# A shorter recurrence step, its inputs by quarters, and five smaller rearrangements in an attention and state-space kernel

## The chip, the cores and the metric

The kernel runs on one core of a Trainium2 chip. The metric is the time of one execution on the device, in microseconds (us). Three runs of the kernel before gave a median of 1029.72 us (1029.02 to 1033.26).

## What is computed

Two blocks follow each other on 512 tokens of width 1024, all in fp32. The first is a gated block: normalisation, one projection into a short convolution and a dilated attention of 8 heads, an output projection, and a feed-forward part of width 2816. The second mixes a state-space model with a sparse attention:

```python
proj = h @ w_in                       # xa, za, q, k, v, zb, qi, ki, wi, ga, gb
ya = gelu(s5_mixer(xa, ...))          # h_t = abar * h_(t-1) + B u_t;  y_t = Re(C h_t) + D u_t
yb = dsa_mixer(q, k, v, qi, ki, wi)   # each query attends to its top 128 keys
merged = sigmoid(ga) * (glu(ya) * silu(za)) @ w_a_o + sigmoid(gb) * (yb * silu(zb)) @ w_b_o
x = x + gate * (merged @ w_out)
return rms_norm_2(x, final_g)
```

The state-space model has 32 groups of 16 channels with 64 complex states each. Abar, the input and output matrices come from parameters through exp, sin and cos, which the kernel computes itself by polynomials.

## The kernel before, in words

**Products.** Every large product is three matmuls of rounded parts (`mm3`, L186 to 190): high by high, high by low, low by high. Weights come in units of 128x1024, 512 KB each. SP loads a unit (`load_w`, L113), ScalarE makes its high part `wh` (L92), VectorE subtracts to get the low part `wl` (L93); three buffers of each kind exist. A projection of one tile of 128 features takes 24 matmuls of 512 columns.

**Order.** TensorE's order is written out by hand: the program mixes a main thread with a "filler", a generator that gives a few k-steps of a projection each time it is called. The orders of the other engines are set by a scheduler from the program, its priorities and its estimate of times. Each engine executes its own order strictly in sequence.

**Start.** `first_w` loads the first weight unit in two pieces of 128x512; the loop at L330 takes the eight tiles of x in turn, splits them, and loads `ident`, `cm`, `lc` and `gqk` at the fifth of them.

**Feed-forward.** For the first gate tiles, exp, sines and tables of the state-space parameters are computed beside the projections (`beside`, with a rate of side work per k-step). The exponentials run as a chain of 128x48 operations on GpSimd (`ex_q`, `ex_r`), the sines on VectorE (`sc_p`); `snr` (L851) joins them. `table` (L884) makes the tiles `ba` and `ca` for four chunks of 8 groups. `gs` (L596) is the gate tile scaled out of PSUM.

**State space.** `ssm_in` projects xa in four quarters, stores each to `xad` in DRAM, and reads all of it back, transposed, as U in eight DMAs. Time is cut in 64 chunks of 8 tokens. `chunk_in` multiplies U by `bt` for each of four sets of 8 groups, copies the four quarters of each result into H (64 chunks x 2 x 16 complex parts), and then runs the recurrence over the chunks: 63 steps of four GpSimd operations (L1136 to L1140), each step needing the one before. Calls of `next(cin)` place the products between q projections (L1160) and heads (L1236). `chunk_out` copies H, shifted by one chunk, into `hs` (L1171) and multiplies by `ca`/`cat` and `tt`. The copies alternate between ScalarE (L241) and VectorE (L243). They are in the filler behind the gate projections `thb` (L1220), while the main thread runs the attention: scores (L249, L250), `z` on VectorE (L253), the exponential `e` on ScalarE (L257), its scaling (L260), transposes (L301), `pT` (L307), values (L278).

**End.** The last projection and the last norm go by halves of 256 tokens. A norm sums squares (L1359, L1362), takes a root on VectorE in a series of 128x2 operations (`rev`, `rey`, L199 to L207), spreads it over partitions (L231) and multiplies eight tiles of x: the first half on GpSimd (L1374), the second on VectorE (L1376).

Of the kernel before, what the change touches and what calls it, by code (L numbers as in the profile page):

```python
# [9 lines left out]
F = mybir.dt.float32  # L10
R = mybir.dt.float32r
# [7 lines left out]
S = 512  # L19
D = 1024  # L20
P = 128
# [7 lines left out]
RAW = 3  # L29
# [5 lines left out]
class K:  # L35
# [8 lines left out]
    def pool(self, st, name, bufs=1, **kw):  # L44
        if "space" not in kw or kw["space"] == PSUM:
            kw.setdefault("reuse_waits", "tile")
        return st.enter_context(self.tc.tile_pool(name=name, bufs=bufs, **kw))


    def setup(self):  # L50
        nc, a, ctx = self.nc, self.a, self.ctx
        c = self.cpool = self.pool(ctx, "consts")
        self.wpool = self.pool(ctx, "weights")
        self.hpool = self.pool(ctx, "parts")
        self.ps = self.pool(ctx, "psum", space=PSUM)
        self.dram = ctx.enter_context(self.tc.tile_pool(name="scratch", bufs=1, space=DRAM))
        self.ones = c.tile([P, P], F, name="ones")
        self.G.memset(self.ones, 1.0)
        warm = c.tile([P, 1], F, name="warm")
        self.A.activation(warm, self.ones[:, 0:1], AF.Tanh)  # L60
        p = self.tp()
        for _ in range(WARM):
            self.T.matmul(p[:, :P], self.ones, self.ones, start=True, stop=True)
        self.cols = c.tile([P, NCOLS], F, name="cols")
        nc.scalar.dma_start(self.cols, a["cols"])
        self.ident = c.tile([P, P], F, name="ident")
        self.ident_r = c.tile([P, P], R, name="ident_r")
        self.cm = c.tile([P, P], F, name="cm")

    def col(self, name, j):  # L70
        o = COLS[name][0] + j
# [23 lines left out]

    def first_w(self):

        raw = self.wpool.tile([P, 2, S], F, name="raw", tag="raw", bufs=RAW)
        hi = self.wpool.tile([P, 2, S], R, name="wh", tag="wh", bufs=3)
        lo = self.wpool.tile([P, 2, S], R, name="wl", tag="wl", bufs=3)  # L100
        for k in range(2):
            src = self.a["wqkv"]
            ap = bass.AP(tensor=src.tensor, offset=src.offset + k * S, ap=[[2 * S, P], [1, S]])
            self.nc.sync.dma_start(raw[:, k], ap)
            self.A.copy(hi[:, k], raw[:, k])
            self.V.tensor_sub(lo[:, k], raw[:, k], hi[:, k].bitcast(F))
            yield hi, lo

    def load_w(self, name, off, kt, n):
        raw = self.wpool.tile([P, kt, n], F, name="raw", tag="raw", bufs=RAW)  # L110
# [5 lines left out]
    def units(self):  # L116

        def cols(name, c0, c1, kt, n):
            for c in range(c0, c1):
                yield self.split_w(self.load_w(name, c * P * kt * n, kt, n))  # L120
        yield from cols("wqkv", 1, 12, 2, S)
        yield from cols("wconv", 0, 12, 8, P)
        yield from cols("wout", 0, 8, 4, 256)
        yield from cols("wgu", 0, 44, 8, P)
        for n in range(8):
            for k0, kt in ((0, 8), (8, 8), (16, 6)):
                yield self.split_w(self.load_w("wdown", (n * 22 + k0) * P * P, kt, P))
        yield from cols("win2", 0, 5, 8, P)
        yield self.split_w(self.load_w("win2v", 0, 8, 72))
        yield from cols("win2", 5, 29, 8, P)  # L130
        yield from cols("wab", 4, 7, 4, 256)
        yield from cols("wglu", 0, 4, 4, 256)
        yield from cols("wab", 7, 8, 4, 256)
        for c in range(4):
            yield from cols("win2", 29 + 2 * c, 31 + 2 * c, 8, P)
            yield from cols("wab", c, c + 1, 4, 256)
        yield from cols("wout2", 0, 8, 8, P)
# [173 lines left out]
    def mixer(self):  # L311
        nc, a, V, A, G, T = self.nc, self.a, self.V, self.A, self.G, self.T
        st = ExitStack()
        sm = self.pool(st, "smallA")
# [13 lines left out]
        sq = sm.tile([P, S], F, name="sqA", tag="sq")  # L328
        first = self.first_w()
        for k in range(8):  # L330
            if k < 2:
                unit = next(first)
                if k:
                    self.ahead.append(unit)
            x = t1.tile([P, S], F, name="x", tag="x", bufs=2)
            nc.sync.dma_start(x, a["xT"][:, k * S:(k + 1) * S])
            if k in (2, 4):
                self.ahead.append(next(self.stream))
            if k == 4:
                nc.sync.dma_start(self.ident, a["ident"])  # L340
                nc.sync.dma_start(self.cm, a["cm"])
                nc.sync.dma_start(self.lc, a["lc"])
                nc.sync.dma_start(self.gqk, a["gqk"])
            g = self.col("g_mix", k)
            A.activation(xh[k], x, AF.Copy, scale=g)
            V.scalar_tensor_tensor(xl[k], x, g, xh[k].bitcast(F), op0=OP.mult, op1=OP.subtract)
            if k == 0:
                A.activation(sq, x, AF.Square)
            else:
                s2 = t1.tile([P, S], F, name="s2", bufs=2)  # L350
                A.activation(s2, x, AF.Square)
                G.tensor_add(sq, sq, s2)
        self.A.copy(self.ident_r, self.ident)
        self.mod_start()
        gqk = sm.tile([P, 64], F, name="gqk1")
        V.scalar_tensor_tensor(gqk, self.gqk[:, 0], 0.125, self.gqk[:, 1], op0=OP.mult, op1=OP.mult)
        rx = sm.tile([P, 4], F, name="rx")
# [207 lines left out]
    def ffn(self, x1):  # L565
# [13 lines left out]
        xs = []  # L579
# [47 lines left out]
        for j in range(22):  # L627
            if j == 0:
                ws, first = [self.w() for _ in range(3)], [self.acc() for _ in range(3)]
                for js, ks in (((0, 1), range(4)), ((2,), range(4)), ((0, 1, 2), range(4, 8))):  # L630
                    for k in ks:
                        for q in js:
                            self.gemm(first[q], ws[q], xs, [k])
                with self.tc.high_priority(offset=LEAD):
                    r = self.rms(wk, [sq], D, "rf")
                continue
            if j == 1:
                first.append(beside(self.proj(xs), 0.25))
                continue
            if j == 2:  # L640
                pg = beside(self.proj(xs, self.acc2), 0.25)
                with self.tc.high_priority(offset=LEAD):
                    Rf = self.spread(wk, r, wk.tile([P, S], F, name="Rf"))
                pu = beside(self.proj(xs, self.acc2), 0.25)
                finish(0, *first[:2])
                finish(1, *first[2:])
                finish(2, pg, pu)
                continue
            ps = []
            for _ in range(2):  # L650
                t = self.proj(xs)
                ps.append(beside(t, 0.25 if j < 4 else 0.36))
            finish(j, *ps)
            if j > NT1:
                self.advance_mod()
# [140 lines left out]
    def ssm_tables(self, st):  # L796
# [84 lines left out]
        for c in range(4):  # L881
            gs = slice(8 * c, 8 * c + 8)
            def table(x, y, nj, name):
# [3 lines left out]
                sh = [P, 8, nj - 1, 16]  # L887
                pw = lambda z: z[:, 1:nj, gs].rearrange("p j g -> p g j")[:, :, :, None].to_broadcast(sh)
                vb = lambda z: z[:, gs, None, :].to_broadcast(sh)
                A.copy(o[:, :, 0], x[:, gs])  # L890
                V.tensor_mul(o[:, :, 1:], vb(x), pw(pr))
                yield
                V.tensor_mul(t, vb(y), pw(pi))
# [95 lines left out]
    def hybrid(self, xs, second, close, out):  # L989
# [35 lines left out]
        ap = self.pool(aa, "attnE")  # L1025
        ss = ExitStack()
        ssp = self.pool(ss, "ssm", side="right")
        U = ssp.tile([P, 32, 64], F, name="U")
        H = ssp.tile([P, 64, 2, 16], F, name="H")
        s1 = ExitStack()  # L1030
# [37 lines left out]
        def ssm_in():  # L1068
            for j in range(4):
# [1 line left out]
                xp = ssi.tile([P, 8, 64], F, name="xp", bufs=2)  # L1071
                A.copy(xp, p.rearrange("p (c s) -> p s c", s=8))
                nc.sync.dma_start(xad[j], xp.rearrange("p s c -> p (s c)"))
            for j in range(8):
                nc.sync.dma_start(U[16 * j:16 * j + 16], x4[7 - j])


        self.filler = ssm_in()
# [41 lines left out]
        def chunk_in():  # L1120
            for c in range(4):
# [5 lines left out]
                pv = pe.rearrange("p (g e c) -> p e g c", e=2, c=64)  # L1127
                for e in range(2):
                    for ri in range(2):
                        self.copy(H[64 * e:64 * e + 64, :, ri, 4 * c:4 * c + 4].rearrange("p c g -> p g c"),  # L1130
                                  pv[64 * ri:64 * ri + 64, e])
                yield
            for c in range(1, 64):
                m = ssi.tile([P, 2, 2, 16], F, name="hm", bufs=2)
# [1 line left out]
                G.tensor_mul(m, H[:, c - 1, None].to_broadcast([P, 2, 2, 16]),  # L1136
                             self.a8.rearrange("p (w r) g -> p w r g", w=2))
                G.tensor_add(u, m[:, 0], H[:, c])  # L1138
                G.tensor_add(H[:, c, 0], u[:, 0], m[:, 1, 1])  # L1139
                G.tensor_add(H[:, c, 1], u[:, 1], m[:, 1, 0])  # L1140


        def silu2(out, p):
# [6 lines left out]
        for c in range(4):  # L1150
            self.filler = self.proj(xs)
            p = None
            for k in range(8):
# [3 lines left out]
                    p = e.value  # L1157
                if k % 2:
                    next(sel, None)
                if k == 7 and c > 1:  # L1160
                    next(cin, None)
            p = self.run(self.filler) if p is None else p
            q.extend(stack(p, 2 * c, 0.125, ap, "q"))
# [69 lines left out]
        def head(i, h):  # L1233
            for _ in range(2 if i < 3 else 0):
                next(sels[min(i + 1, 2)], None)
            if i == 0 and h < 3:  # L1236
                next(cin, None)
            if h == 0:
                for m in range(i):
# [114 lines left out]
        def norm(e):  # L1354
# [15 lines left out]
                Rs = x3p.tile([P, S // 2], F, name="Rs")  # L1370
                A.copy(Rs, Rl)
            for k in range(8):
                if e == 0:
                    G.tensor_mul(x3[k][:, t], x3[k][:, t], Rs)  # L1374
                else:
                    V.tensor_mul(x3[k][:, t], x3[k][:, t], Rl)  # L1376
                if k % 2:
                    nc.sync.dma_start(out.rearrange("(k p) t -> p k t", p=P)[:, k - 1:k + 1, t],
                                      x3t[:, k - 1:k + 1, t])
# [1 line left out]
        for n in range(5, 8):  # L1381
            self.run(last(n, 0))
        self.run(last(5, 1))
        first, second = norm(0), norm(1)
        next(first)
        next(first)
        self.run(last(6, 1))
        b = last(7, 1)
        for _ in range(4):
            next(b)  # L1390
        next(second)
        for _ in range(2):
            next(b)
        self.run(first)
        self.run(b)
        self.run(second)
        st.close()
# [97 lines left out]
```

## Time and profile before

| | |
|---|---|
| median of the runs | 1029.72 us |
| profiled execution | 1028.98 us |
| its span | 1027.20 us |
| TensorE (PE) busy | 993.3 us, 97% of the span |
| VectorE (DVE) busy | 686.9 us, 67% |
| ScalarE (ACT) busy | 423.1 us, 41% |
| GpSimd (POOL) busy | 168.5 us, 16% |
| mean granted clock of TensorE | 0.988 |

The span is what the profile covers; 1.78 us of the profiled execution lie around it. Busy times of engines overlap, so they don't add up. TensorE is named PE, VectorE DVE, ScalarE ACT, GpSimd POOL and SyncE SP in the rows; a row gives the line of the kernel in the listing, and the last bracket the idle time before the instruction with what ended it. "x8" at a row's end says that eight like instructions in a row are shown as one.

### The profile page before, as it was taken

How to read it: one execution, taken by the hardware profiler on the slowest of the kernel's cores; microseconds unless marked ns; L12 is line 12 of the kernel's file. 1: busy time of each engine (PE TensorE's matmuls, PEld its weight loads, DVE VectorE, ACT ScalarE, POOL GpSimd, SP SyncE). 2: the span in 40 equal slices, each digit the busy share in tenths (PEclk: the TensorE clock that was granted, in tenths of full speed). 3: DMA queues.
4: the chain of work that ended last, by engine and by line, in shares of the span. 5: the costliest groups of instructions: out<-in, count | busy, mean ns of one | idle time of the engine just before them, and what ended most of it. 6: DMA issues, size and time to landing. Idle time of an engine off the chain costs nothing.

```text
span 1027.2 us, 13898 instructions
## 1 busy us (share of the span) xinstructions
PE 993.3 (97%) x5074; PEld 824.6 (80%) x5074; DVE 686.9 (67%) x1315; ACT 423.1 (41%) x717; POOL 168.5 (16%) x393
## 2 busy tenths in 40 slices
PE   9999999999999999999999999999997699999995
PEld 7788887888777778888888898888886687888884
DVE  4876788786898747778642267799984455644434
ACT  6445555533344333323222235544443464333251
POOL 3021111007700000000011000001888200000022
PEclk9999999999999999999999999999999799999997
DMA  7233221123245556554634342273222254422212
GB/s 265 82 118 130 82 72 53 57 88 127 82 139 161 159 178 234 176 190 161 208 130 132 100 141 84 103 143 103 84 83 103 71 156 103 163 105 102 82 42 82
DMA packets 55572, 125.12 MB, mean 122 GB/s; under 512 B 17424, under 2 KB 24080, under 8 KB 55376
## 3 DMA queue, kind: packets, MB, share of 16 engines
q1 hardware_dynamic: 55360, 124.19, 37.0%
q8 instruction: 40, 0.66, 0.3%
q14 instruction: 28, 0.23, 0.1%
q10 hardware_dynamic: 144, 0.05, 0.0%
HBM read 110.45 MB, written 12.58 MB: 120 GB/s over the span
## 4 chain that ended last, share of the span: by engine, by line
PE 75%; POOL 10%; DVE 6%; DMA 3%; issue 3%; ACT 2%; SPq 1%; ACTq 0%; DVEq 0%; POOLq 0%
PE acc L188 20%; PE acc L189 20%; PE acc L190 20%; POOL hm L1136 2%; PE acc L370 2%; PE acc L368 2%; PE acc L369 2%; POOL hu L1138 2%; POOL H L1139 2%; POOL H L1140 2%; PE acc L278 1%; PE tp L301 1%; DVE wl L93 1%; SPq L1195 1%; DMA yl<-yad 1%
## 5 line engine op out<-in xcount | busy, mean ns | idle before, releaser
L92 ACT CAST wh<-raw 128x1024 fp32r<-128x1024 f32 x157 | 162.5, 1036 | 279.2 <-PE acc L189 233.2
L93 DVE TENSOR_TENSOR wl<-raw,wh 128x1024 fp32r<-128x1024 f32 x157 | 195.0, 1243 | 88.2 <-ACT wh L92 86.7
L188 PE MATMUL acc<-fh,wh 128*128 128x512 f32 x336 | 133.1, 396 | 1.0 <-DVE gs L596 1.0
L189 PE MATMUL acc<-fl,wh 128*128 128x512 f32 x336 | 130.9, 390 | 0.0
L190 PE MATMUL acc<-fh,wl 128*128 128x512 f32 x336 | 130.9, 389 | 0.0
L188 PE MATMUL acc<-hh,wh 128*128 128x512 f32 (+1 forms) x280 | 111.4, 398 | 0.0
L190 PE MATMUL acc<-hh,wl 128*128 128x512 f32 (+1 forms) x280 | 109.5, 391 | 0.0
L189 PE MATMUL acc<-hl,wh 128*128 128x512 f32 (+1 forms) x280 | 109.4, 391 | 0.0
L188 PEld LDWEIGHTS acc<-fh,wh 128*128 128x128 f32 x336 | 63.1, 188 | 15.9 <-issue 1.9
L190 PEld LDWEIGHTS acc<-fh,wl 128*128 128x128 f32 x336 | 63.1, 188 | 13.4
L189 PEld LDWEIGHTS acc<-fl,wh 128*128 128x128 f32 x336 | 63.1, 188 | 12.8 <-issue 0.2
L188 PE MATMUL acc<-th,wh 128*128 128x512 f32 (+1 forms) x198 | 72.6, 367 | 0.0
L189 PE MATMUL acc<-tl,wh 128*128 128x512 f32 (+1 forms) x198 | 72.3, 365 | 0.0
L190 PE MATMUL acc<-th,wl 128*128 128x512 f32 (+1 forms) x198 | 72.3, 365 | 0.0
L257 ACT ACTIVATE e<-z,mn 128x128 f32<-128x128 f32 (+3 forms) x64 | 36.0, 563 | 70.9 <-DVE mn L253 70.8
L190 PEld LDWEIGHTS acc<-hh,wl 128*128 128x128 f32 (+1 forms) x280 | 52.2, 186 | 12.0
L188 PEld LDWEIGHTS acc<-hh,wh 128*128 128x128 f32 (+1 forms) x280 | 52.2, 187 | 10.2 <-issue 0.7
L189 PEld LDWEIGHTS acc<-hl,wh 128*128 128x128 f32 (+1 forms) x280 | 52.3, 187 | 9.6
L1136 POOL TENSOR_TENSOR hm<-H,a 128x64 f32<-128x64 f32 x63 | 23.9, 379 | 125.8 <-DVE H L243 120.9
L677 POOL TENSOR_TENSOR sqD<-sqD,s 128x512 f32<-128x512 f32 x6 | 8.4, 1398 | 209.5 <-ACT s L664 209.5
L188 PEld LDWEIGHTS acc<-th,wh 128*128 128x128 f32 x198 | 37.3, 189 | 6.1
L189 PEld LDWEIGHTS acc<-tl,wh 128*128 128x128 f32 x198 | 37.3, 189 | 6.1
(402 smaller groups left out, 2137.2 us busy)
## 6 DMA issues: line engine op xcount, KB each, us to landing
raw<-in_wgu SPq DMA_DIRECT2D x44, 512.0 KB, 3.5
raw<-in_win SPq DMA_DIRECT2D x37, 512.0 KB, 3.5
mraw<-in_wmod SPq DMA_DIRECT2D x24, 512.0 KB, 4.8
raw<-in_wout SPq DMA_DIRECT2D x16, 512.0 KB, 3.4
raw<-in_wdown SPq DMA_DIRECT2D x16, 512.0 KB, 3.6
raw<-in_wconv SPq DMA_DIRECT2D x12, 512.0 KB, 3.4
raw<-in_wqkv SPq DMA_DIRECT2D x11, 512.0 KB, 4.1
x<-in_xT SPq DMA_DIRECT2D x16, 256.0 KB, 5.4
```

Of the source, the lines that this page charges most:

```text
L92: self.A.copy(hi, raw)
L93: self.V.tensor_sub(lo, raw, hi.bitcast(F))
L188: self.T.matmul(out, lh, rh, start=start, stop=False)
L189: self.T.matmul(out, lh, rl, start=False, stop=False)
L190: self.T.matmul(out, ll, rh, start=False, stop=stop)
L257: self.A.activation(e[:, :n], z[:, :n], AF.Exp, bias=mn, scale=-1.0, accum_out=den)
L368: T.matmul(ps[i], xh[k][:, t], wh[:, kk], start=k == 0, stop=False)
L369: T.matmul(ps[i], xh[k][:, t], wl[:, kk], start=False, stop=False)
L370: T.matmul(ps[i], xl[k][:, t], wh[:, kk], start=False, stop=k == 7)
L1136: G.tensor_mul(m, H[:, c - 1, None].to_broadcast([P, 2, 2, 16]), self.a8.rearrange("p (w r) g -> p w r g", w=2))
L1138: G.tensor_add(u, m[:, 0], H[:, c])
L1139: G.tensor_add(H[:, c, 0], u[:, 0], m[:, 1, 1])
```

## The change

1. In the recurrence, the two additions into H (one for the real, one for the imaginary part) become one of 32 columns, whose second operand is read in reverse order of its middle axis.
2. U is read back in quarters, each behind its own store, in 8 DMAs of a quarter each. `chunk_in` is called at the end of q projections 0, 1 and 2 and in the middle of projection 3, instead of after 2 and 3 and beside heads 0 to 2; the copies into H are all on ScalarE.
3. Four pools get a padding tile so that the next pool begins at a multiple of 512 bytes; GpSimd clears it.
4. The first two weight units are loaded in pieces of 128x512, x gets a third buffer, and the constants are loaded with the last tile of x.
5. In the feed-forward part, the side work is taken out of gate tiles 1 and 2 and put into tile 3; the first column block of `ba` and `ca` is copied on GpSimd instead of ScalarE.
6. At the end, the first half's multiplications go from GpSimd to VectorE, and its spread comes two k-steps earlier than the second half's first sums.

```diff
     def first_w(self):
-        raw = ...; hi = ...; lo = ...
-        for k in range(2):
...
+        for c in range(2):
+            raw = self.wpool.tile([P, 2, S], F, name="raw", tag="raw", bufs=RAW)
...
+            for k in range(2):
+                ap = bass.AP(tensor=src.tensor, offset=src.offset + (c * P * 2 + k) * S, ap=[[2 * S, P], [1, S]])
...
-            x = t1.tile([P, S], F, name="x", tag="x", bufs=2)
+            x = t1.tile([P, S], F, name="x", tag="x", bufs=3)
...
-            if k in (2, 4):
+            if k == 4:
                 self.ahead.append(next(self.stream))
-            if k == 4:
+            if k == 7:
                 nc.sync.dma_start(self.ident, a["ident"])
...
             if j == 1:
-                first.append(beside(self.proj(xs), 0.25))
+                first.append(self.run(self.proj(xs)))
...
-                ps.append(beside(t, 0.25 if j < 4 else 0.36))
+                ps.append(beside(t, 0.7 if j < 4 else 0.36))
...
-                A.copy(o[:, :, 0], x[:, gs])
+                G.tensor_copy(o[:, :, 0], x[:, gs])
...
+        self.pad(ssp, 480)
...
                 nc.sync.dma_start(xad[j], xp.rearrange("p s c -> p (s c)"))
-            for j in range(8):
-                nc.sync.dma_start(U[16 * j:16 * j + 16], x4[7 - j])
+                for s in range(8):
+                    nc.sync.dma_start(U[16 * s:16 * s + 16, 8 * j:8 * j + 8], x4[7 - s][:, 8 * j:8 * j + 8])
...
-                        self.copy(H[64 * e:64 * e + 64, :, ri, 4 * c:4 * c + 4].rearrange("p c g -> p g c"),
+                        A.copy(H[64 * e:64 * e + 64, :, ri, 4 * c:4 * c + 4].rearrange("p c g -> p g c"),
...
-                G.tensor_add(H[:, c, 0], u[:, 0], m[:, 1, 1])
-                G.tensor_add(H[:, c, 1], u[:, 1], m[:, 1, 0])
+                G.tensor_add(H[:, c], u, m[:, 1, ::-1])
...
-                if k == 7 and c > 1:
+                if k == (3 if c == 3 else 7):
                     next(cin, None)
...
-            if i == 0 and h < 3:
+            if i == 0 and h == 0:
                 next(cin, None)
...
-                if e == 0:
-                    G.tensor_mul(x3[k][:, t], x3[k][:, t], Rs)
-                else:
-                    V.tensor_mul(x3[k][:, t], x3[k][:, t], Rl)
+                V.tensor_mul(x3[k][:, t], x3[k][:, t], Rl if e else Rs)
...
         b = last(7, 1)
-        for _ in range(4):
-            next(b)
-        next(second)
         for _ in range(2):
             next(b)
         self.run(first)
+        for _ in range(2):
+            next(b)
+        next(second)
```

ScalarE, beside the attention of the second block. `e` is the exponential of a head's scores, `pT` the transposed result, `thb` a gate projection, `hs` the input of the recurrence's output. Before:

```order
L1220 ACTIVATE thb_6439<-acc 128x512
L307 COPY pT<-tp 128x384
L257 ACTIVATE e,den<-z,mn 128x384
L307 COPY pT<-tp 128x384
L257 ACTIVATE e,den<-z,mn 128x384
L92 CAST wh<-raw 128x1024
L1220 ACTIVATE thb_6440<-acc 128x512
L257 ACTIVATE e,den<-z,mn 128x384
L307 COPY pT<-tp 128x384 x2
L257 ACTIVATE e,den<-z,mn 128x384
L241 COPY hs<-H 64x4x63 x2
L92 CAST wh<-raw 128x1024
```

and in the changed kernel:

```order
L97 CAST wh<-raw 128x1024
L263 ACTIVATE e,den<-z,mn 128x384
L1227 ACTIVATE thb_6501<-acc 128x512
L247 COPY hs<-H 64x4x63 x2
L313 COPY pT<-tp 128x256
L263 ACTIVATE e,den<-z,mn 128x384
L313 COPY pT<-tp 128x256
L97 CAST wh<-raw 128x1024
L263 ACTIVATE e,den<-z,mn 128x384
L1227 ACTIVATE thb_6502<-acc 128x512
```

The copies of `hs` moved ahead: before, they follow gate projection `thb` number 3 (of 0 to 7) and the exponentials of two heads behind it, now they follow number 1 at once.

GpSimd in the first exponential of the state-space parameters; `ca` is a table tile, `bc` its input from VectorE. Before:

```order
L754 TENSOR_TENSOR ex_k<-ex_k,ex_i 128x48
L756 TENSOR_SCALAR ex_f<-ex_i 128x48
L748 TENSOR_SCALAR ex_q<-ex_r 128x48
L730 TENSOR_SCALAR stt<-ex_q 128x48
L731 TENSOR_TENSOR ex_q<-stt,ex_r 128x48
```

and in the changed kernel:

```order
L763 TENSOR_SCALAR ex_f<-ex_i 128x48
L755 TENSOR_SCALAR ex_q<-ex_r 128x48
L897 COPY ca<-bc 128x8x16
L737 TENSOR_SCALAR stt<-ex_q 128x48
L738 TENSOR_TENSOR ex_q<-stt,ex_r 128x48
```

A copy from the table stands inside the chain.

VectorE where that chain is joined; `snr` needs the exponential, `wl` is a weight split, `gs` the first gate tile. Before:

```order
L851 TENSOR_SCALAR snr<-pr 128x48
L855 TENSOR_TENSOR sw<-pi,tab 128x48
L854 TENSOR_TENSOR scr<-snr,tab 128x48
L859 TENSOR_TENSOR sci<-pi,tab 128x48
L93 TENSOR_TENSOR wl<-raw,wh 128x1024
L856 TENSOR_TENSOR scr<-scr,sw 128x48
L596 TENSOR_TENSOR gs<-acc,Rf 128x512
```

and in the changed kernel:

```order
L858 TENSOR_SCALAR snr<-pr 128x48
L98 TENSOR_TENSOR wl<-raw,wh 128x1024
L862 TENSOR_TENSOR sw<-pi,tab 128x48
L861 TENSOR_TENSOR scr<-snr,tab 128x48
L866 TENSOR_TENSOR sci<-pi,tab 128x48
L603 TENSOR_TENSOR gs<-acc,Rf 128x512
```

The weight split moved ahead of three of the small operations, directly behind `snr`.

## Rows read from the trace of the kernel before

**Rows 1.** TensorE's waits: engine, line <- releaser: total us, times, longest.
```profile
PE acc L1183 <- POOL hs L1171: 13.2, 1, 13.2
...
PE tp L231 <- DVE rey L205: 5.4, 2, 5.0
...
PE acc L188 <- DVE gs L596: 1.0, 1, 1.0
```

**Rows 2.** Timeline of TensorE, 777 to 805: start us, us, engine, line, op, out<-in.
```profile
777.76 0.82 PE L301 MATMUL tp<-ident,e 128*128 128x128 f32 x6
...
804.08 0.69 PE L1183 MATMUL acc<-hs,cat 128*128 128x64 f32 x2 [13.20 <-POOL hs L1171]
```

**Rows 3.** Windows: us, busy time (count) of each engine, granted clock, DMA share, GB/s.
```profile
804.00:809.00 5.00, 4.92 (x35) 4.42 (x36) 2.09 (x5) 2.60 (x6) 0.03 (x1) 0.55 0.29 105
```

**Rows 4.** Timeline of GpSimd, 717 to 722, two steps.
```profile
717.50 0.32 POOL L1136 TENSOR_TENSOR hm<-H,a 128x64 f32<-128x64 f32 x1
...
717.90 0.25 POOL L1138 TENSOR_TENSOR hu<-hm,H 128x32 f32<-128x32 f32 x1
...
718.23 0.22 POOL L1139 TENSOR_TENSOR H<-hu,hm 128x16 f32<-128x16 f32 x1
...
718.71 0.33 POOL L1136 TENSOR_TENSOR hm<-H,a 128x64 f32<-128x64 f32 x1
...
720.66 1.21 POOL L1139 TENSOR_TENSOR H<-hu,hm 128x16 f32<-128x16 f32 x1
```

**Rows 5.** Timeline of VectorE, 720 to 722.
```profile
720.57 1.21 DVE L93 TENSOR_TENSOR wl<-raw,wh 128x1024 fp32r<-128x1024 f32 x1
```

**Rows 6.** Timeline of TensorE, 691 to 694.
```profile
691.96 1.89 PE L1126 MATMUL acc<-U,bt 128*128 128x64 f32 x16
...
693.66 0.48 PE L188 MATMUL acc<-hh,wh 128*128 128x512 f32 x1
```

**Rows 7.** Timeline of VectorE, 713 to 716.
```profile
713.48 0.65 DVE L243 COPY H<-acc 64x256 f32<-64x256 f32 x1
```

**Rows 8.** Timeline of ScalarE, 770 to 803.
```profile
770.23 0.58 ACT L1220 ACTIVATE thb<-acc 128x512 f32<-128x512 f32 x1
...
802.24 1.25 ACT L241 COPY hs<-H 64x252 f32<-64x252 f32 x2 [12.38 <-POOL H L1139]
```

**Rows 9.** Timeline of GpSimd, 238 to 264.
```profile
240.47 0.33 POOL L748 TENSOR_SCALAR ex_q<-ex_r 128x48 f32<-128x48 f32 x1
```

**Rows 10.** Timeline of VectorE, 241 to 268.
```profile
241.46 0.48 DVE L878 TENSOR_SCALAR bc<-bc,sg 128x512 f32<-128x512 f32 x1 [3.72 <-DMA sg<-in_sgn]
...
262.82 0.26 DVE L851 TENSOR_SCALAR snr<-pr 128x48 f32<-128x48 f32 x1 [3.87 <-POOL pr L822]
...
265.06 0.68 DVE L596 TENSOR_TENSOR gs<-acc,Rf 128x512 f32<-128x512 f32 x1
```

**Rows 11.** Timeline of TensorE, 5 to 34.
```profile
5.38 0.79 PE L368 MATMUL acc<-wh,xh 128*128 128x512 f32 x1 [0.60 <-ACT xh L345]
...
32.93 0.39 PE L369 MATMUL acc<-wl,xh 128*128 128x512 f32 x1
...
33.39 1.02 PE L214 MATMUL tp<-sqA,ones 128*128 128x512 f32 x2
```

**Rows 12.** Timeline of GpSimd, 1008 to 1028.
```profile
1012.93 5.49 POOL L1374 TENSOR_TENSOR x<-x,Rs 128x256 f32<-128x256 f32 x8 [16.79 <-ACT Rs L1371]
```

**Rows 13.** Timeline of VectorE, 1008 to 1028.
```profile
1015.83 0.58 DVE L199 TENSOR_SCALAR rev<-res 128x2 f32<-128x2 f32 x1
...
1018.47 0.16 DVE L204 TENSOR_TENSOR ret<-rev,rey 128x2 f32<-128x2 f32 x1
...
1021.14 2.73 DVE L1376 TENSOR_TENSOR x<-x,tp 128x256 f32<-128x256 f32 x8 [1.38 <-PE tp L231]
```

**Rows 14.** Instructions of line 188, 875 to 975: ns min/median/max, first and last start.
```profile
L188 PE MATMUL acc<-hh,wh x64: 389/389/398, 899.0 to 958.5; 128*128 128x512 f32 x64
...
L188 PE MATMUL acc<-yah,wh x32: 394/394/398, 909.9 to 964.0; 128*128 128x512 f32 x32
```

More of the change, by code (lines that the diff above doesn't have):

```diff
@@ L47, in pool, with pad @@
         return st.enter_context(self.tc.tile_pool(name=name, bufs=bufs, **kw))
+    def pad(self, pool, size):
+        self.G.memset(pool.tile([P, size // 4], F, name="pad"), 0.0)
     def setup(self):
@@ L68, in setup @@
         self.cm = c.tile([P, P], F, name="cm")
+        self.pad(c, 96)
     def col(self, name, j):
@@ L96, in first_w @@
     def first_w(self):
-        raw = self.wpool.tile([P, 2, S], F, name="raw", tag="raw", bufs=RAW)
-        hi = self.wpool.tile([P, 2, S], R, name="wh", tag="wh", bufs=3)
-        lo = self.wpool.tile([P, 2, S], R, name="wl", tag="wl", bufs=3)
-        for k in range(2):
[L102 to L107, printed above, removed]
+        src = self.a["wqkv"]
+        for c in range(2):
+            raw = self.wpool.tile([P, 2, S], F, name="raw", tag="raw", bufs=RAW)
+            hi = self.wpool.tile([P, 2, S], R, name="wh", tag="wh", bufs=3)
+            lo = self.wpool.tile([P, 2, S], R, name="wl", tag="wl", bufs=3)
+            for k in range(2):
+                ap = bass.AP(tensor=src.tensor, offset=src.offset + (c * P * 2 + k) * S, ap=[[2 * S, P], [1, S]])
+                self.nc.sync.dma_start(raw[:, k], ap)
+                self.A.copy(hi[:, k], raw[:, k])
+                self.V.tensor_sub(lo[:, k], raw[:, k], hi[:, k].bitcast(F))
+                yield hi, lo
     def load_w(self, name, off, kt, n):
@@ L120, in cols @@
                 yield self.split_w(self.load_w(name, c * P * kt * n, kt, n))
-        yield from cols("wqkv", 1, 12, 2, S)
+        yield from cols("wqkv", 2, 12, 2, S)
         yield from cols("wconv", 0, 12, 8, P)
@@ L330, in mixer @@
         for k in range(8):
-            if k < 2:
+            if k < 4:
                 unit = next(first)
-                if k:
+                if k % 2:
                     self.ahead.append(unit)
-            x = t1.tile([P, S], F, name="x", tag="x", bufs=2)
+            x = t1.tile([P, S], F, name="x", tag="x", bufs=3)
             nc.sync.dma_start(x, a["xT"][:, k * S:(k + 1) * S])
-            if k in (2, 4):
+            if k == 4:
                 self.ahead.append(next(self.stream))
-            if k == 4:
+            if k == 7:
                 nc.sync.dma_start(self.ident, a["ident"])
@@ L354, in mixer @@
         self.mod_start()
+        self.pad(sm, 448)
         gqk = sm.tile([P, 64], F, name="gqk1")
@@ L637, in ffn @@
             if j == 1:
-                first.append(beside(self.proj(xs), 0.25))
+                first.append(self.run(self.proj(xs)))
                 continue
             if j == 2:
-                pg = beside(self.proj(xs, self.acc2), 0.25)
+                pg = self.run(self.proj(xs, self.acc2))
                 with self.tc.high_priority(offset=LEAD):
                     Rf = self.spread(wk, r, wk.tile([P, S], F, name="Rf"))
-                pu = beside(self.proj(xs, self.acc2), 0.25)
+                pu = self.run(self.proj(xs, self.acc2))
                 finish(0, *first[:2])
@@ L1129, in chunk_in @@
                     for ri in range(2):
-                        self.copy(H[64 * e:64 * e + 64, :, ri, 4 * c:4 * c + 4].rearrange("p c g -> p g c"),
-                                  pv[64 * ri:64 * ri + 64, e])
+                        A.copy(H[64 * e:64 * e + 64, :, ri, 4 * c:4 * c + 4].rearrange("p c g -> p g c"),
+                               pv[64 * ri:64 * ri + 64, e])
                 yield
@@ L1383, in hybrid @@
         self.run(last(5, 1))
+        self.pad(x3p, 352)
         first, second = norm(0), norm(1)
```

## The prediction

> **What bounds the kernel now.** I read the waits of TensorE first, since it works in nearly the whole span: a change can only gain where TensorE stands still or runs slowly. Three of its waits matter here [rows 1]: 13.2 us for the inputs `hs` of the recurrence's output, 5.0 us in the longest wait for a `rey` (the last norm), 1.0 us for `gs` of the first gate tile. The timeline round the longest shows where it lies [rows 2]: TensorE does attention scores until 790.9 and resumes with `hs` at 804.08. The windows show what follows: in the 5 us after the resumption the granted clock is 0.55 [rows 3], between the two levels 1.2 and 2.4 GHz, so 5.0 x 0.45 = 2.25 us more are lost. The gap costs 15.5 us in all, twice every other wait together.
>
> Then I read GpSimd's and the neighbours' timelines to see why `hs` is late. The recurrence is 63 steps in series on GpSimd. A step goes by starts hm 717.50, hu 717.90, the first H 718.23, next hm 718.71: 0.40 + 0.33 + 0.48 = 1.21 us, both H in the 0.48 [rows 4]. One row there lasts 1.21 instead of 0.22 us, 0.09 us after VectorE began a weight split `wl` [rows 4, 5]; 12 such stalls stand in the recurrence, 0.97 us each. It starts when the last state copy of chunk 3 ends, 713.48 + 0.65 = 714.1 [rows 7]: 714.2 + 63 x 1.21 + 12 x 0.97 = 802.1, and ScalarE's `hs` copies start at 802.24 after 12.4 us of waiting [rows 8].
>
> **The change part by part.** All sums start from the profiled execution, 1028.98 us (span 1027.20 and 1.78 around it); the median of the runs is 0.74 above it.
>
> *Earlier start.* Before, the first chunk product stands at 691.96, behind projection 2, and takes 1.70 until projection 3 starts at 693.66 [rows 6]; two follow that projection and one a later head. Now chunks 0 to 2 stand behind projections 0 to 2, and chunk 3 in the middle of projection 3. Two more products stand ahead of projection 3: 693.66 + 2 x 1.70 = 697.06, plus half of its 24 matmuls at 0.23 (the distance of two successive ones [rows 11]) = 699.8. The product ends at 701.5, and four copies, now all on ScalarE, cost 4 x 0.64 = 2.6 (duration of the VectorE copy [rows 7]): start about 704.3, 9.9 us earlier. The product itself is moved, not added, and costs TensorE nothing. The 32 short U loads on SP instead of 8 stand behind each xad store; weights are issued behind them, covered by three weight buffers; without that cover, one would be late by a microsecond or two.
>
> *Three operations.* The two H additions on 16 columns become one on 32, reading one operand backwards. No row shows a backward operand. hu has 32 columns as the new H, and takes 0.33 from start to start [rows 4]; so 0.48 becomes 0.33 and the step 1.06. From below, no dearer than one 16-column H: 0.22 and the 0.08 between hu's end (718.15) and H's start, 0.30, a step of 1.03. From above, nothing gained: 1.21; dearer still is a rival. I take 1.06, the nearest row. 63 x 1.06 = 66.8, and 11 stalls of 0.97 = 10.7, as no `wl` runs at the end: the recurrence ends at 704.3 + 66.8 + 10.7 = 781.8, against 802.1.
>
> In sentences that the sum does not need: the Trainium skill, SBUF — State Buffer, section "Who interferes with whom", says a VectorE instruction with two SBUF inputs contends with a GpSimd instruction that reads SBUF. The stalled row agrees. By that rule dropping one of four operations removes no stall, since a stall belongs to a `wl`; only fewer `wl` in a shorter window do.
>
> *Where `hs` stands.* It does not follow that 20 us are gained. ScalarE and VectorE execute in order, and the copies `hs` now stand far ahead: on ScalarE behind `thb` number 1 of 0 to 7 (770.23 to 770.81 in the trace of before [rows 8]), ahead of an exp and two `pT` copies that attention needs. Both engines would reach the copies at about 771 and 772, and wait until 781.8. Queued behind them are the exp and normalisation of the second head of a pair; TensorE runs on until it needs these, the transposes at 777.76 [rows 2]. After the recurrence ScalarE does two `hs` copies (1.25 [rows 8]), a `pT` copy, the exp, then VectorE reciprocal and scaling: about 3.3 us. TensorE thus stands from 777.8 to 785.1: 7.3 us in place of 13.2; the later `hs` products wait for nothing. Gain 5.9. The stall is still long, so I leave the low clock behind it as it was. Ends: the recurrence done by 774.5 takes the whole 15.5; a step of 1.21 ends it at 791.2, stall 16.7, 3.5 slower.
>
> *First block.* The copy `ca` moves to GpSimd and there stands behind `ex_q` (240.47, done 240.80 [rows 9]); its input `bc` is ready at 241.94 [rows 10]. So the GpSimd chain waits 1.1 and copies some 0.5 (estimated between hm on 64 columns, 0.32 [rows 4], and double that): 1.6 later. VectorE's `snr` at 262.82 waited for this chain [rows 10], and now a `wl` stands between `snr` and the next operations too: `gs`, 265.06 before, comes at about 266.5. TensorE's 1.0 us wait for it becomes 2.5: +1.5, ends 0 and +2.5. The other sine work now stands beside one gate tile; VectorE's order hardly moves by it, so I cost it at nothing. VectorE's own work covers it; if the weight splits in that order come late, TensorE waits there.
>
> *Start.* The 108 matmuls from 5.38 to 33.39 take 28.0 us; at 0.23 from one to the next, as at 32.93 and 33.39 (two matmuls in 0.46), they would take 24.8 [rows 11]. So at most 3.2 is to be had from weights and x that come earlier, and part of it no load gives back: the first matmul lasts 0.79. I take -0.7, ends -3.2 and +0.5, because the bytes are the same and only their order differs, with `ident`, `cm`, `lc` behind them.
>
> *End.* Eight multiplications leave GpSimd (5.49 us from 1012.93 [rows 12]). Under them four tiny VectorE operations take 1018.47 - 1015.83 = 2.64 us; without, at the 0.16 of their neighbour [rows 13] spaced at 0.2, about 0.7: -1.9. The `Rs` spread now stands earlier on TensorE and waits 0.6 for `rey`, and eight VectorE multiplications (2.73 for eight [rows 13]) fit ahead of the last x: +0.6, and the rest is hidden. I take -1.4, ends -2.5 and 0.
>
> *Beginnings on 512 bytes.* No row names a beginning. The same matmul lasts 389 ns on `hh` and 394 on `yah` [rows 14], 5 ns that a beginning may or may not explain. If all 512-column matmuls from 875 to 975, about 430 at 0.23 us, lost 5 ns, it would be 2.2 us; a loss of that size by moved tiles can't be excluded either. I take -0.5, between nothing and the gain: ends -2.2 and +2.2.
>
> Sum: -5.9 + 1.5 - 0.7 - 1.4 - 0.5 = -7.0, so 1022.0 us.
>
> **The rivals.** *A: the recurrence is done before anybody waits.* For it speaks that 9.9 us of head start and 9.5 us of shorter steps are large against a 13.2 us gap; against it the early place of `hs`, which moves the deadline from 790.9 to about 774.5. It needs a step of (774.5 - 704.3 - 10.7) / 63 = 0.94, or almost no stalls. Then gap and clock loss go: 1028.98 - 15.5 + 1.5 - 0.7 - 1.4 - 0.5 = 1012.4.
>
> *B: slower, because the backward operand is dear.* The mechanism is one GpSimd instruction, in series 63 times, with two engines parked behind it. The stall equals the old 13.2 when the recurrence ends at 787.7, which is a step of 1.15. Above 1.15 each 0.1 costs 6.3 us; were H to hold 0.58 instead of 0.33, the step is 1.31, the end 797.5, the stall 23.0: +9.8, and with the small terms (-1.1) 1037.7. For it: no backward reading is in the trace, and the move of attention ahead of it takes away the slack that hid 13 us. Against it: hm, with twice the columns and a broadcast operand, lasts only 0.32.
>
> *C: the wait changes place and nothing else.* The step stays near 1.15, the start is gained, the early `hs` gives it back: -1.1 from the small terms alone, 1027.9; with more of the first block's delay, 1029 to 1030.
>
> **How the numbers follow.** About 0.5% of the time, 5 us, is what a measurement can tell from no change: the borders are 1024.6 and 1034.9. The forecast has 0.55 (1017 to 1027; some 0.08 of it above 1024.6), A 0.18, C 0.18, B 0.09. Faster: 0.47 + 0.18 and a little of C's near side, 0.67; same 0.24; slower 0.09. For 8 in 10 the range takes A's time below and C's above, leaving B and the far side of A: 1012 to 1029.5. All of the likeliest case lies in 1017 to 1027.
>
> **What would show it.** GpSimd: three rows a step, spaced 1.06, from about 704 to 782. TensorE's waits: no 13 us for `hs`, but some 7 us for transposes of `e` near 778 to 785, released by VectorE. ScalarE idle 10 us ahead of `hs`. `gs` wait of 2.5 us; in the last norm rows of 0.16 instead of 0.65. It is wrong if the step is not near 1.06, if no wait of TensorE stands near 780, or if waits appear in 275 to 310 or before 34 us that rows of before don't have.

## The result, and the profile after

The changed kernel took 1022.93 us (median of five runs, 1021.21 to 1024.96), against 1033.26 of the kernel before in the same comparison (1029.02 to 1034.76): a ratio of 0.991, 95% interval 0.990 to 0.993. The forecast of 1022.0 (1012.0 to 1029.5), faster by over 0.5%, held. The profiled execution took 1022.29 us with a span of 1020.6, 6.6 less than before. The medians lie 10.3 us apart: the five runs of the kernel before spread over 5.7 us, and its profiled execution, 1028.98 us, is as fast as the fastest of them, so the pair of profiles shows the smaller difference.

TensorE's waits after, the longest first (engine, line <- releaser: total, times, longest):

```profile
PE tp L307 <- ACT pT L313: 5.2, 1, 5.2
PE tp L237 <- DVE rey L211: 4.0, 3, 3.2
PE tp L237 <- DVE sc_p L795: 1.8, 1, 1.8
PE tp L915 <- ACT bts L916: 1.3, 1, 1.3
...
PE acc L194 <- DVE gs L603: 1.1, 1, 1.1
```

The 13.2 us for `hs` [rows 1] are gone; at the top stands a wait of 5.2 us for a copy `pT`. `rey` fell from 5.0 to 3.2, `gs` hardly moved, and `bts` is new. GpSimd's timeline in the changed kernel, the first steps and one stalled:

```profile
707.01 0.32 POOL L1144 TENSOR_TENSOR hm<-H,a 128x64 f32<-128x64 f32 x1 [111.31 <-ACT H L1138]
707.41 0.25 POOL L1146 TENSOR_TENSOR hu<-hm,H 128x32 f32<-128x32 f32 x1
707.75 0.25 POOL L1147 TENSOR_TENSOR H<-hu,hm 128x32 f32<-128x32 f32 x1
708.08 0.32 POOL L1144 TENSOR_TENSOR hm<-H,a 128x64 f32<-128x64 f32 x1
...
709.14 1.26 POOL L1144 TENSOR_TENSOR hm<-H,a 128x64 f32<-128x64 f32 x1
```

A step lasts 708.08 - 707.01 = 1.07 us, where it was 1.21 [rows 4]; the addition that reads backwards takes 0.25, as long as hu. The last row is a stalled one; 11 such stand in this recurrence, 12 before. The recurrence starts 7.2 us earlier than 714.2. Now ScalarE and TensorE at the place where the rest is decided:

```profile
772.59 0.58 ACT L1227 ACTIVATE thb<-acc 128x512 f32<-128x512 f32 x1
783.90 1.25 ACT L247 COPY hs<-H 64x252 f32<-64x252 f32 x2 [10.73 <-POOL H L1147]
785.05 0.36 ACT L313 COPY pT<-tp 128x256 f32<-128x256 f32 x1
785.44 0.61 ACT L263 ACTIVATE e<-z,mn 128x384 f32<-128x384 f32 x1
```

```profile
785.46 0.90 PE L307 MATMUL tp<-ident,e 128*128 128x128 f32 x3 [5.16 <-ACT pT L313]
786.94 0.87 PE L307 MATMUL tp<-ident,e 128*128 128x128 f32 x3 [0.57 <-DVE e L266]
```

ScalarE reaches `hs` at 773.2, idles 10.7 us, and only then makes the `pT` and the `e` for which TensorE stands, 5.16 + 0.57 = 5.7 us. Behind it the granted clock is low, as behind the old gap [rows 3]. The windows (length, busy time of PE, PEld, DVE, ACT, POOL with counts, granted clock, DMA share, GB/s), of the kernel before, then of the changed one:

```profile
804.00:808.00 4.00, 3.92 (x26) 3.59 (x28) 2.09 (x5) 2.60 (x6) 0.03 (x1) 0.50 0.26 90
808.00:812.00 4.00, 4.00 (x38) 3.74 (x34) 0.70 (x2) 0.23 (x1) 0.00 (x0) 0.94 0.10 41
```

```profile
786.00:788.00 2.00, 1.43 (x7) 0.76 (x7) 1.68 (x5) 1.99 (x7) 0.00 (x0) 0.50 0.00 0
788.00:790.00 2.00, 2.00 (x17) 1.67 (x16) 1.50 (x6) 1.68 (x6) 0.00 (x0) 0.50 0.23 41
790.00:792.00 2.00, 2.00 (x6) 1.56 (x6) 1.35 (x6) 0.31 (x1) 0.00 (x0) 0.54 0.58 225
```

Busy time multiplied by what the clock lacks gives a loss of some 2.2 us before and 2.9 us after (with the half microsecond of work ahead of 786).

Where the 6.6 us lie is read from the starts of the same matmul in both traces (us):

| stretch, by a matmul at its end | before | after | difference so far | of the stretch |
|---|---|---|---|---|
| start, `sqA,ones` | 33.39 | 32.26 | -1.13 | -1.1 |
| `tp<-ident,rxy` | 183.72 | 184.05 | +0.33 | +1.5 |
| first gate tile's wait, `acc<-fh,wh` | 265.79 | 266.69 | +0.90 | +0.6 |
| tables, `mhi,ones_r` | 417.59 | 419.86 | +2.27 | +1.4 |
| recurrence, `acc<-ybh,wh` | 852.81 | 848.30 | -4.51 | -6.8 |
| last merge, `acc<-mh,wh` | 964.73 | 959.68 | -5.05 | -0.5 |
| last spread, `ident,rey` | 1019.90 | 1013.37 | -6.53 | -1.5 |

### The profile page after: what moved, and what is told of

Its sections match the earlier page's. It is cut to its first block, busy times and chain, and to the rows that moved or that the text cites. A ratio compares the mean times of both kernels' runs of the same rounds, so it can differ in the third digit from the quotient of the medians.

```text
span 1020.6 us, 13878 instructions
## 1 busy us (share of the span) xinstructions
PE 993.8 (97%) x5074; PEld 826.2 (81%) x5074; DVE 689.3 (68%) x1316; ACT 426.2 (42%) x718; POOL 160.8 (16%) x334
## 4 chain that ended last, share of the span: by engine, by line
PE 75%; POOL 8%; DVE 6%; DMA 4%; issue 3%; ACT 2%; SPq 2%; ACTq 0%; DVEq 0%; POOLq 0%
PE acc L194 19%; PE acc L195 19%; PE acc L196 19%; POOL hm L1144 3%; PE acc L375 2%; PE acc L376 2%; PE acc L377 2%; POOL H L1147 2%; POOL hu L1146 2%; DVE wl L98 2%; PE acc L284 1%; PE tp L307 1%; DMA yl<-yad 1%; SPq L1202 1%; DMA sg<-in_sgn 1%
## 5 line engine op out<-in xcount | busy, mean ns | idle before, releaser
L1144 POOL TENSOR_TENSOR hm<-H,a 128x64 f32<-128x64 f32 x63 | 27.0, 429 | 116.2 <-ACT H L1138 111.3
L196 PEld LDWEIGHTS acc<-th,wl 128*128 128x128 f32 x198 | 37.3, 189 | 6.0
```

The lines of the kernel that those rows point to most:

```text
L196: self.T.matmul(out, ll, rh, start=False, stop=stop)
```

## The experiments

Ratios are to the kernel before, run on the same chip in the same comparison; the brackets are 95% intervals.

**The place of hs.** The changed kernel with one edit; the lists `ths` and `wls`, which record the gate projections on ScalarE and the weight splits on VectorE as they are issued, are left out here:

```diff
...
+            with ExitStack() as after:
+                if c == 0:
+                    after.enter_context(self.tc.issue_after(self.ths[3]))
+                    after.enter_context(self.tc.issue_after(self.wls[-1]))
+                for e in range(2):
...
```

> The changed kernel with one thing altered: the copies of hs for chunk 0 are queued behind gate projection thb number 3 on ScalarE and behind the last weight split before them on VectorE, instead of behind thb number 1. Theory (the waiting copies, being early in two engines' orders, hold up attention's exponentials): the recurrence ends at about 785 as before, or one weight-split stall (0.97 us) later, both engines work on until about 787 to 789, TensorE needs hs at about 793; the waits of 5.2 and 0.6 us at 780 to 787 vanish and so does the half clock behind them (about 2.5 us): 8 us less than the changed kernel, about 1014.5. Rival (the recurrence's end is the limit wherever the copies stand): the wait appears again before the product of hs and cat, no more than 1 us is gained, about 1022.

1013.35 us, ratio 0.982 [0.979, 0.985]. Every wait of TensorE between 776 and 808 is gone. ScalarE's copies start at once, and the clock stays full:

```profile
787.98 0.59 ACT L1232 ACTIVATE thb<-acc 128x512 f32<-128x512 f32 x1
788.47 1.35 ACT L247 COPY hs<-H 64x252 f32<-64x252 f32 x2
789.84 0.62 ACT L263 ACTIVATE e<-z,mn 128x384 f32<-128x384 f32 x1
```

```profile
785.00:790.00 5.00, 5.00 (x27) 4.29 (x26) 2.94 (x8) 3.52 (x7) 2.04 (x9) 1.00 0.01 2
790.00:795.00 5.00, 5.00 (x28) 4.30 (x27) 3.12 (x11) 3.17 (x8) 0.00 (x0) 1.00 0.28 105
```

The early place of the waiting copies cost the changed kernel some 9 us, as much as the whole change had gained. The theory holds, its rival falls, and this version beats both kernels. The edit moves the copies on ScalarE and VectorE at once, so this run does not tell the two engines apart.

**The shorter step alone**, on the kernel before:

```diff
-                G.tensor_add(H[:, c, 0], u[:, 0], m[:, 1, 1])
-                G.tensor_add(H[:, c, 1], u[:, 1], m[:, 1, 0])
+                G.tensor_add(H[:, c], u, m[:, 1, ::-1])
```

> The kernel before with the three-operation step alone. Theory: steps of 1.06 us from 714.2, ended at about 791 instead of 802; the scheduler now puts hs behind thb number 2 and two pT copies on ScalarE (about 780), so TensorE stands from about 785 to 794 for transposes instead of 13.2 us for hs: 3 to 4 us less than the kernel before. Rival (the step's saving goes through in full): 62 steps of 0.15 us, 9 us less.

1027.09, ratio 0.996 [0.994, 0.997], 4 to 5 us less. The scheduler moved `hs` ahead here too, and TensorE's waits show the exchange, with a new one for U:

```profile
PE tp L301 <- DVE e L260: 7.2, 1, 7.2
PE tp L231 <- DVE rey L205: 5.4, 2, 5.0
...
PE acc L1126 <- DMA U<-xad: 1.4, 1, 1.4
```

The theory's mechanism and size hold. The `e` that TensorE waits for is normalised on VectorE, behind VectorE's own `hs` copies:

```profile
792.39 0.82 DVE L243 COPY hs<-H 64x252 f32<-64x252 f32 x2 [12.50 <-POOL H L1139]
793.71 0.41 DVE L260 TENSOR_SCALAR e<-e,rd 128x384 f32<-128x384 f32 x1
```

Why U came 1.4 us late, with its loads not edited, stays open.

**The earlier start alone**, on the kernel before: U by quarters, the earlier products, all copies into H on ScalarE. Two of its four places:

```diff
...
-                        self.copy(H[...], pv[...])
+                        A.copy(H[...], pv[...])
...
-                if k == 7 and c > 1:
+                if k == (3 if c == 3 else 7):
...
```

> The kernel before with the regrouped U, the earlier products and ScalarE's copies alone, four operations a step. Theory: the recurrence starts 7 us earlier (707), ends at about 793.5; hs stands behind thb number 2, so TensorE waits from about 785 to 797 for transposes: 1 to 2 us less than the kernel before. Rival (the earlier start goes through in full): 7 us less.

1024.84, ratio 0.993 [0.990, 0.995], 7 us less: the theory's 1 to 2 us are wrong, and the rival's size is right. The recurrence starts at 706.68 as expected, but TensorE gets past the transposes before it is stopped by a score:

```profile
787.25 0.82 PE L301 MATMUL tp<-ident,e 128*128 128x128 f32 x6
...
795.74 0.69 PE L249 MATMUL sc<-kh,q 128*128 128x384 f32 x1 [5.58 <-DVE mn L253]
```

A wait of 5.6 instead of 13.2 is 7.6 less. I had put the stop at the transposes. On ScalarE `hs` stands where it stands in the run before, behind `thb` number 2, an exponential and two `pT` copies; the difference is VectorE's order, in which `hs` now comes behind the normalisation of that `e`:

```profile
781.66 0.42 DVE L260 TENSOR_SCALAR e<-e,rd 128x384 f32<-128x384 f32 x1
...
794.25 0.83 DVE L243 COPY hs<-H 64x252 f32<-64x252 f32 x2 [11.38 <-POOL H L1140]
```

So VectorE's place of `hs` counts as ScalarE's does. The two halves alone bring about 4.8 and 7.0 us, together in the changed kernel less than their sum.

**Both factors crossed.** Late `hs` with four operations a step, and late `hs` with the shorter step on the kernel before:

> hs_late with four operations a step again. In hs_late the last part of H that hs needs is ready at about 786.5, the copies start at 788.5 without waiting and TensorE uses them at 794.2. Theory: 62 steps by 0.15 us more end at about 796, TensorE stands 4 to 6 us before the hs product or the transposes next to it, with up to 2.5 us of half clock behind: 1018 to 1021. Rival (once the copies stand late, the step's length is hidden): the same as hs_late, 1013.4.

1019.98, ratio 0.988 [0.986, 0.990].

```profile
795.16 0.43 PE L1195 MATMUL acc<-hs,cat 128*128 128x64 f32 x2 [3.38 <-POOL hs L1179]
```

> three_alone with the copies of hs for chunk 0 held behind thb number 3, as in hs_late. Theory (the shorter step passes through once no exponential stands behind the waiting copies): the recurrence ends at about 793, the hs product starts at about 795 instead of 804, a wait of about 4 us instead of 13.2, 9 us less than the kernel before, up to 11 if the clock stays high: 1018 to 1021. Rival (the place of the copies makes no difference): as three_alone, 1027.

1020.70, ratio 0.989 [0.986, 0.992].

```profile
795.21 0.47 PE L1186 MATMUL acc<-hs,cat 128*128 128x64 f32 x2 [3.07 <-POOL hs L1170]
```

In both the recurrence decides again, by a 3 us wait for `hs` itself, with a low clock behind it (0.71 from 798 to 802 in the first). So with the copies late, the step is worth 1019.98 - 1013.35 = 6.6 us by medians of two comparisons, and the late place is worth 1027.09 - 1020.70 = 6.4 us to the shorter step alone. The waits of 3.4 and 3.1 are somewhat below the 4 us expected; the cause stays open.

The profiles allow the same comparison for the stretch of the recurrence alone, from the first `mhi,ones_r` to the first `ybh,wh`, without the scatter of the rest of the kernel:

| stretch of the recurrence, us | four operations a step | three |
|---|---|---|
| old start, `hs` where the scheduler puts it | 435.2 (before) | 431.2 (three_alone) |
| early start, `hs` where the scheduler puts it | 427.7 (early_alone) | 428.5 (the changed kernel) |
| old start, `hs` late | not run | 425.7 (three_late) |
| early start, `hs` late | 425.5 (late_four) | 419.8 (hs_late) |

With the early start and the scheduler's order the shorter step brings nothing, with `hs` late 5.7 us; the late place brings the changed kernel 8.7 us.

**Padding out.** The changed kernel without the four `pad` lines.

> The changed kernel without the four padding tiles. Theory (a matmul's duration goes by where its operands begin): the matmuls on sh, mh and ybh last 394 ns again as in the kernel before, 389 with the padding; some 150 matmuls by up to 5 ns, 0.4 to 0.7 us slower than the changed kernel, less than a comparison can tell. Rival (the 5 ns come from something else that the change moved): 389 ns stay.

1025.23, ratio 0.993 [0.990, 0.996]: in time not to be told from the changed kernel. In the trace the durations (ns min/median/max, of the first of three products) go up again; after, then without padding:

```profile
L194 PE MATMUL acc<-sh,wh x27: 389/389/389, 870.2 to 887.9; 128*128 128x512 f32 x27
L194 PE MATMUL acc<-mh,wh x16: 389/389/397, 959.7 to 969.9; 128*128 128x512 f32 x16
```

```profile
L193 PE MATMUL acc<-sh,wh x24: 393/394/395, 870.1 to 885.9; 128*128 128x512 f32 x24
L193 PE MATMUL acc<-mh,wh x18: 391/394/399, 957.8 to 969.7; 128*128 128x512 f32 x18
```

So 4 to 5 ns go with the padding on `sh` and `mh`. From one start to the next the matmuls on `sh` take 227 ns with it and 231 without, those on `mh` and its low part `ml` 227 and 233: over some 180 matmuls about 1 us, where I had expected 0.4 to 0.7. On `ybh`, which I had counted in, the distance changes by less than 1 ns, and on `yah` the matmuls last 394 ns in both.

**Tables and sines.** Two single undos of the changed kernel; then hs_late with both undone.

```diff
-                G.tensor_copy(o[:, :, 0], x[:, gs])
+                A.copy(o[:, :, 0], x[:, gs])
```

> The changed kernel with the first column block of ba and ca copied on ScalarE again. In question: the new wait of 1.25 us at 326 of the transposes of ba for ScalarE's bts. Theory (the table work begins earlier, because the side work stands in gate tile 3, and the buffer that bts needs is still being stored): the wait stays, 1.2 us; only the exponential chain gets shorter by 1.3 us, and gs waits 0.2 to 1.0 us less. Rival (GpSimd's copies make the tables late): the 1.25 us wait goes. In all 0 to 1.5 us less than the changed kernel.

1022.66, ratio 0.992 [0.990, 0.994]. In time it is not to be told from the changed kernel. The wait for `bts` stays at 1.3 us, so GpSimd's copies alone don't cause it. `gs` waits 1.5 instead of 1.1, `sc_p` 1.0 instead of 1.8: not what I expected of `gs`, in sum 0.4 less.

```diff
-                first.append(self.run(self.proj(xs)))
+                first.append(beside(self.proj(xs), 0.25))
...
-                ps.append(beside(t, 0.7 if j < 4 else 0.36))
+                ps.append(beside(t, 0.25 if j < 4 else 0.36))
```

> The changed kernel with the side work at rate 0.25 beside gate tiles 1 to 3 as before. Theory: the tables stand where they stood, the wait for bts at 326 goes: 1.2 us less; the wait for gs stays near 1.1. Rival: the 1.25 us wait stays, as GpSimd's copies cause it.

1022.82, ratio 0.992 [0.989, 0.994]. Again the time is that of the changed kernel. The wait at 326 goes (0.4 us remain at 304): the side work in the third tile causes it. In the changed kernel `bts` waited for a store that holds its buffer:

```profile
325.82 0.59 ACT L916 COPY bts<-tp 128x512 f32<-128x512 f32 x1 [4.85 <-DMA tabs<-tt]
```

> hs_late with the side work and the ScalarE copies of the tables as before. Theory: the waits of hs_late for bts (1.6 us) goes, those for sc_p and gs shrink by 0.3 each: 1.5 to 2 us less than hs_late, about 1011.5. Rival: those waits were hidden anyway, same as hs_late, 1013.4.

1013.39, ratio 0.983 [0.980, 0.985], the same as hs_late: the rival's time holds. The `bts` wait is gone. The stretch from the first gate tile's wait to the tables takes 151.8 us, as in the kernel before; it is 153.2 in the changed kernel and in tab_act, 152.5 in side_old, 153.5 in hs_late. So the trace gains 1.7 us there on hs_late, and only both undos together bring the stretch back. The wait for `sh` grew from 1.1 to 2.4 us, which takes the gain back in this profile, but that is not shown to come from the edit: between the changed kernel and end_pool below, whose orders agree up to the last norm, the same wait differs as much. The changed kernel, then end_pool:

```profile
PE acc L194 <- ACT sh L1208: 0.9, 1, 0.9
```

```profile
PE acc L194 <- ACT sh L1208: 2.2, 1, 2.2
```

Why the gain does not show in the times stays open.

**The end.** The changed kernel with the first half's eight multiplications on GpSimd again.

> The changed kernel with the eight multiplications of the first half on GpSimd again, the earlier spread kept. Theory (GpSimd's operations and the tiny VectorE operations of the root hold each other up): the multiplications start about 1.5 us earlier than in the kernel before, so only the ones still running meet the root; one to three of its first four operations take 0.6 us instead of 0.17: TensorE's wait for rey grows from 3.2 us to 3.7 to 4.7. Rival (the shorter rows came from the earlier spread): all rows stay at 0.17, wait 3.2.

1023.21, ratio 0.991 [0.989, 0.994]; the wait for `rey` stays at 3.2, and from the first `mh,wh` to the last spread it takes 53.7 us as in the changed kernel (55.2 before). GpSimd and VectorE in this run:

```profile
1008.81 5.53 POOL L1380 TENSOR_TENSOR x<-x,Rs 128x256 f32<-128x256 f32 x8 [15.15 <-ACT Rs L1378]
```

```profile
1014.43 0.17 DVE L205 TENSOR_SCALAR rev<-res 128x2 f32<-128x2 f32 x1
1014.63 0.17 DVE L206 TENSOR_SCALAR rey<-rev 128x2 int32<-128x2 int32 x1
```

The rival holds: the earlier spread alone lets GpSimd end at 1014.34, 0.09 us ahead of the root. In the kernel before, under GpSimd's work, these rows took 0.58 to 0.65 ([rows 13], and the second of them here), beside no such work 0.17. The move to VectorE added nothing.

```profile
1016.44 0.65 DVE L200 TENSOR_SCALAR rey<-rev 128x2 int32<-128x2 int32 x1
```

## Why the prediction was right, point by point

The likeliest case came: the mechanism forecast, early copies of `hs` that hold up the attention's exponentials, is what the trace shows and what hs_late removes. That the sum of -7.0 us meets the 6.6 us of the profiles within half a microsecond is in part luck: a low clock ahead of 184 that stood in no term cost 1.5 us and the first block 0.5 more than forecast, while the recurrence brought 0.9 and the start 0.4 more.

- **Step.** 1.06 forecast, 1.07 measured, with the 11 stalls forecast. Rival B, the dear backward operand, is refuted: 0.25 us.
- **Start.** Forecast 704.3 in the old trace's time; TensorE stands 2.3 later there after the stretches up to the tables, so 706.6, and 707.0 was measured.
- **Place of `hs`.** This term carried the forecast and is shown by hs_late. Forecast: copies free at 781.8 (784.1 with the shift), measured 783.9; the start is 0.4 later and the steps add up to 0.6 more, but `hs` takes H only up to the last step but one, which I had missed. Stall 7.3, measured 5.7: it ended 0.5 us sooner than forecast, began 0.2 later, and has 0.9 us of transposes inside it. Those are the first head's; they waited for a free `tp`, which a `pT` copy behind `hs` had to empty, and only then came the wait for the second head's `e`. The low clock behind the stall, which I had left as it was, costs 0.7 us more. So 7.5 less of waiting makes -6.8 in the stretch, against -5.9. That the gap was "twice every other wait together" is wrong: the others in that list add up to 14.3 us. No term rests on it.
- **Rival A** needed a step of 0.94 with `hs` early; what brought its 1012.4 was another place of `hs`, 1013.35 in hs_late. **Rival C** is refuted by the step and by the 6.8 us.
- **First block.** The step that failed in size: TensorE's wait for `gs` was to grow by 1.5, and it grew by 0.1, from 1.0 to 1.1. The chain lost 1.0 us instead of 1.6 (`snr` comes 1.3 later, 0.3 of it already there at 184), and `gs` follows `snr` 0.4 sooner, as an `scr` operation left its way. The +0.6 of the stretch lies mostly in the wait for `sc_p` ahead of it, 1.3 before and 1.8 after; `gs` is 0.6 later too, but TensorE comes later to meet it.

```profile
258.95 1.13 PE L237 MATMUL tp<-ident,rfy 128*128 128x128 f32 x8 [1.78 <-DVE sc_p L795]
```

```profile
264.11 0.26 DVE L858 TENSOR_SCALAR snr<-pr 128x48 f32<-128x48 f32 x1 [4.44 <-POOL pr L829]
...
265.96 0.68 DVE L603 TENSOR_TENSOR gs<-acc,Rf 128x512 f32<-128x512 f32 x1
```

  What I cost at nothing, the sines in the third tile, made a wait of 1.25 us for `bts`; side_old removes that wait, but no time shows a gain from it. I had looked for late weight splits there, and not for a buffer held by a store.
- **Start of the kernel.** -1.1 against -0.7. At the same matmul the four profiles with the old loads stand at 33.2 to 34.1, the eight with the new ones at 30.6 to 33.1: the new loads are earlier, by 1.6 on the mean, but one pair of profiles doesn't give the size. Which of the edits to the loads does it was not tried.
- **End.** -1.5 against -1.4; right in size, but I gave the move to VectorE the credit that belongs to the earlier spread.
- **Beginnings.** -0.5 taken, about 1 us by the distances between matmuls, too little for a comparison of times.
- **The +1.5 before 184** stood in no step; it is told below.

## What to carry to other kernels

When a producer gets faster, look at where the scheduler puts its consumer: an engine that executes in order and reaches a waiting copy early holds up everything behind it, and here that cost as much as the faster producer gained. Order such a copy behind the last work that must not wait, then measure again; the shorter step was worth its 6 us only then. Look at every engine that has a part of the consumer: here, with the same order on ScalarE, VectorE's decided whether TensorE stopped at the transposes. Two improvements of one chain don't add up, and a wait that goes from a trace (`bts`) need not show in the time.

## What the runs showed of the hardware that was not expected

- Two waits of TensorE, of 0.6 to 0.7 and 1.2 us, stand between 166 and 173 in every profile. In five of twelve (the changed kernel, hs_late, early_alone, end_pool, best_old_sides) the granted clock then fell to 0.5 for some us; in the other seven it stayed at 1.00. From `sqc,ones` to `rxy` TensorE takes 11.1 to 11.2 us without and 11.9 to 12.4 with it. The changed kernel:

```profile
170.00:174.00 4.00, 3.76 (x8) 2.30 (x9) 1.68 (x6) 0.81 (x2) 0.00 (x0) 0.58 0.02 6
```

  What decides it stays open; it accounts for the +1.5 in this pair of profiles, and may for part of the spread of the runs, which no run separates. The wait for `sh` is a second such place: it lasts 0.5 to 2.4 us, and in six of the twelve (three_alone, early_alone, late_four, tab_act, end_pool, best_old_sides, all with 1.4 us or more) the clock fell behind it, while three_late kept 1.00 behind 1.8 us. From `ybh,wh` to `mh,wh` TensorE takes 111.1 to 112.5 us without and 113.7 to 115.6 with it.
- A 128x32 addition on GpSimd costs 0.25 us with one operand read backwards, as without; two of 16 columns took 0.22 each.
- Matmuls of 512 columns on the same tiles (`sh`, `mh`) last 389 ns with the padding and 393 to 394 without. That the place where the tiles begin does it is what the padding was meant for; no row shows a beginning.
